# First feed-forward block of a decoder trunk: raw tokens enter, the RMS scale is applied behind the first products

## The chip, the cores and the metric

The kernel runs on one core of one Trainium2 chip. The metric is the device time of one execution in microseconds; the kernel before takes 1079.5 us (median of three runs, 1079.46 to 1080.34).

## The reference, cut to what matters

One layer of a hybrid decoder: feed-forward, token mixer, feed-forward, on 16 meta tokens and 512 real tokens of width 1024. The change is in the first feed-forward alone:

```python
def rms_norm(x, g):
    ms = jnp.mean(xf * xf, axis=-1, keepdims=True)
    return xf * lax.rsqrt(ms + EPS) * g

def swiglu(h, w_in, w_out):
    gate, up = jnp.split(h @ w_in, 2, axis=-1)
    return (jax.nn.silu(gate) * up) @ w_out

h = jnp.concatenate([pad, meta, x], axis=1)
h = h + 0.5 * swiglu(rms_norm(h, ffn1_norm), ffn1_w_in, ffn1_w_out)   # d_ff = 2816
```

Two things follow from these lines. The factor 1/rms belongs to a token, so it can be put on a token's column of the product `h @ w_in` as well as on the token itself. And the sum needs the raw `h` a second time, as the residual.

## The kernel before, in words

**Numbers and products.** Everything is float32. TensorE works on "fp32r" operands, so each matrix is split into a high part (a rounded copy, made by ScalarE in `hi`, L134/L135) and a low part (the remainder, made by VectorE in `lo`, L141/L143). One product is then three matmuls: high by high (L302), low by high (L303), high by low (L305), 128 x 128 weights against 264 columns of tokens. Weights are split in the same way as they come in (`raw` to `wh` and `wl`).

**Layout.** Activations stand turned, features on partitions and 528 tokens (16 + 512) along the row: `hT` is 128 x 8 x 528. The tokens come in five tiles `xt` (one of 16, four of 128 tokens), are turned by TensorE's transposes (L668) into PSUM tiles called `ps` and `pt`, and are copied out in two halves: the first 264 columns are "token 0", the last 264 "token 1"; features 0 to 511 and 512 to 1023 are the two feature halves. A11, A12, A21, A22 are the four blocks (token, feature).

**Units.** The first projection is done in 22 units of 128 gate columns and 128 up columns. Units 0 and 1 are "plain" (`Units.plain`, L482): 8 block products each, that is 96 matmuls a unit and 192 in the two. Units 2 to 21 use seven products in place of eight (`Units.seven`, L519, 84 matmuls); they need sums of the blocks, made by `Halves.sums` (L434): S3 = A11 - A21, S1 = A21 - A22, S2 = S1 - A11, S4 = A12 + S2, each a 128 x 1056 VectorE operation and then split in two parts of 128 x 1056. Their weights come as sums too, part of which the accumulating DMA of GpSimd's queue (L212) forms, and part VectorE (`tc`, L234 and L235).

**The entry before.** A token tile is squared and summed (L635, L636), 1/rms comes from a small VectorE operation (`entry_rms`, L650) and a power on GpSimd (L352), and the tile is scaled in place (`entry_scale`, L660) before it is turned. So `hT` holds normalised tokens (with the gain), and the raw tokens are loaded a second time while units 4 to 6 run (`fetch`, L795) and turned again to become the residual (`residual` and `turn`, L810 to L819: 40 transposes and 10 copies). TensorE runs 20 matmuls on an identity matrix first (L346) while the loads are under way.

**What sets the order.** A scheduler orders each engine's instructions when the program is built, from the order of the code and from the buffers; on the chip each engine takes its queue strictly in that order, and waits at an instruction whose operands or buffers aren't ready. `inline` (L619) ties entry operations of one engine to each other. PSUM has four `ps` and four `pt` tiles. The weight tiles `raw`, `wh` and `wl` have three buffers each, the tiles for added weights (`rawC`, `rawD`) two.

## Time and profile before

| what | value |
|---|---|
| median of three runs | 1079.5 us |
| the profiled execution's own time | 1080.09 us |
| its span, first to last instruction | 1078.3 us |
| mean granted TensorE clock | 1.000 |
| busy: TensorE, VectorE, ScalarE, GpSimd | 1069.0, 893.2, 656.6, 195.9 us |
| TensorE's share of the chain that ended last | 89% |

In the profile PE is TensorE's matmuls, PEld its weight loads, DVE VectorE, ACT ScalarE, POOL GpSimd, and SP the engine that issues most loads. A row of the timeline gives start, duration, engine, line, operation, tiles and count; a part in brackets is idle time before it and what ended it. Durations overlap by some hundredths of a microsecond on a busy engine, so the step from one start to the next is an instruction's cost there; for a matmul of 264 columns, whose row says 0.28 us, that step is about 0.122 us.

### The profile page before, as it was taken

Reading aid. Unit: us, or ns where it says so; the run is one execution under the profiler, and the core shown is the slowest. Engines: PE = TensorE matmul, PEld = TensorE weight load, DVE = VectorE, ACT = ScalarE, POOL = GpSimd, SP = SyncE. Lnnn points to the kernel's source line nnn. Section 1 sums busy time; section 2 is a strip of 40 time slices with the busy share of each in tenths; the row PEclk is TensorE's granted clock in tenths of the full one; section 3 lists DMA queues with packets and bytes.
Section 4 is the critical chain, followed back from the end, with each engine's and each line's share of the span. In section 5 each row is a group of like instructions: output and inputs, shape, how many; then the busy total and the mean of one; then the engine's idle time right before and its main releaser. Section 6 shows DMA issues by size and latency. Waiting matters only on the chain.

```text
span 1078.3 us, 22318 instructions
## 1 busy us (share of the span) xinstructions
PE 1069.0 (99%) x8579; PEld 1037.4 (96%) x8579; DVE 893.2 (83%) x1718; ACT 656.6 (61%) x1243; POOL 195.9 (18%) x233
## 2 busy tenths in 40 slices
PE   9999999999999999999999999999999999999998
PEld 8999999999999999999978799999999999999998
DVE  7988878888889677788897799788998788887895
ACT  7667456656666455556667866555666466645664
POOL 3011111121124430221200110001122211221120
PEclk9999999999999999999999999999999999999999
DMA  7787788688786423112211775467688777887763
GB/s 267 212 213 166 189 192 196 152 222 213 177 179 174 121 75 124 48 53 74 74 52 60 232 178 139 173 199 199 174 203 176 191 187 184 180 192 193 161 123 103
DMA packets 111723, 173.06 MB, mean 160 GB/s; under 512 B 10800, under 2 KB 58160, under 8 KB 111232
## 3 DMA queue, kind: packets, MB, share of 16 engines
q1 hardware_dynamic: 74032, 122.03, 35.9%
q0 software_dynamic: 28768, 37.83, 22.6%
q10 hardware_dynamic: 8816, 11.77, 3.3%
q8 instruction: 67, 1.10, 0.4%
q14 instruction: 40, 0.33, 0.1%
HBM read 167.37 MB, written 6.32 MB: 161 GB/s over the span
## 4 chain that ended last, share of the span: by engine, by line
PE 89%; DVE 6%; ACT 3%; issue 1%; DMA 1%; POOL 0%; ACTq 0%; SPq 0%; DVEq 0%; POOLq 0%
PE ps L302 15%; PE ps L305 15%; PE ps L303 15%; PE pt L302 12%; PE pt L303 12%; PE pt L305 12%; DVE wl L141 1%; ACT t L1189 1%; ACT wh L134 1%; DMA raw<-in_wg_dram 1%; PE ps L346 1%; DVE pL L141 1%; PE pt L1229 1%; PE pt L1274 1%; PE ps L1396 0%
## 5 line engine op out<-in xcount | busy, mean ns | idle before, releaser
L302 PE MATMUL ps<-x,wh 128*128 128x256 f32 (+2 forms) x768 | 219.7, 286 | 0.2
L303 PE MATMUL ps<-x,wh 128*128 128x256 f32 (+2 forms) x768 | 218.9, 285 | 0.5 <-DVE x L143 0.4
L305 PE MATMUL ps<-x,wl 128*128 128x256 f32 (+2 forms) x768 | 218.9, 285 | 0.0
L141 DVE TENSOR_TENSOR wl<-raw,wh 128x1024 fp32r<-128x1024 f32 (+3 forms) x125 | 150.1, 1202 | 44.5 <-ACT wh L134 43.2
L134 ACT CAST wh<-raw 128x1024 fp32r<-128x1024 f32 (+3 forms) x125 | 128.5, 1029 | 88.0 <-PE ps L303 57.4
L302 PEld LDWEIGHTS ps<-x,wh 128*128 128x128 f32 x768 | 144.8, 189 | 1.7 <-ACT hT L687 0.3
L303 PEld LDWEIGHTS ps<-x,wh 128*128 128x128 f32 x768 | 144.5, 188 | 1.4 <-DVE x L143 0.9
L305 PEld LDWEIGHTS ps<-x,wl 128*128 128x128 f32 x768 | 144.6, 188 | 0.9
L302 PE MATMUL pt<-x,wh 128*128 128x256 f32 (+2 forms) x424 | 125.3, 296 | 0.2 <-ACT wh L134 0.2
L305 PE MATMUL pt<-x,wl 128*128 128x256 f32 (+2 forms) x424 | 124.5, 294 | 0.0
L303 PE MATMUL pt<-x,wh 128*128 128x256 f32 (+2 forms) x392 | 112.5, 287 | 0.0
L134 ACT CAST wh<-tc 128x1024 fp32r<-128x1024 f32 (+1 forms) x70 | 71.8, 1026 | 64.5 <-DVE tc L235 57.1
L141 DVE TENSOR_TENSOR wl<-tc,wh 128x1024 fp32r<-128x1024 f32 (+1 forms) x70 | 83.5, 1193 | 32.4 <-ACT wh L134 32.1
L302 PE MATMUL ps<-acts,wh 128*128 128x264 f32 (+1 forms) x352 | 100.5, 285 | 0.1
L305 PE MATMUL ps<-acts,wl 128*128 128x264 f32 (+1 forms) x352 | 99.9, 284 | 0.0
L303 PE MATMUL ps<-acts,wh 128*128 128x264 f32 (+1 forms) x352 | 99.5, 283 | 0.0
L141 DVE TENSOR_TENSOR wl<-rawC,wh 128x1024 fp32r<-128x1024 f32 (+1 forms) x70 | 84.2, 1202 | 5.8 <-ACT wh L134 5.5
L134 ACT CAST wh<-rawC 128x1024 fp32r<-128x1024 f32 (+1 forms) x70 | 71.6, 1023 | 22.8 <-PE pt L303 17.8
L302 PEld LDWEIGHTS pt<-x,wh 128*128 128x128 f32 x424 | 79.9, 189 | 2.6 <-ACT wh L134 0.5
L305 PEld LDWEIGHTS pt<-x,wl 128*128 128x128 f32 x424 | 79.7, 188 | 2.1
L303 PEld LDWEIGHTS pt<-x,wh 128*128 128x128 f32 x392 | 73.8, 188 | 0.6
L302 PEld LDWEIGHTS ps<-acts,wh 128*128 128x128 f32 x352 | 66.5, 189 | 0.7 <-DVE h2T L919 0.3
(427 smaller groups left out, 3248.4 us busy)
## 6 DMA issues: line engine op xcount, KB each, us to landing
rawC<-in_w1i_dram SPq DMA_DIRECT2D x20, 512.0 KB, 4.7
raw<-in_w1i_dram SPq DMA_DIRECT2D x40, 256.0 KB, 4.7
raw<-in_w2i_dram SPq DMA_DIRECT2D x40, 256.0 KB, 3.4
rawC<-in_w2i_dram SPq DMA_DIRECT2D x20, 512.0 KB, 4.4
raw<-in_wm_dram SPq DMA_DIRECT2D x18, 512.0 KB, 4.5
raw<-in_wout_dram SPq DMA_DIRECT2D x16, 512.0 KB, 4.1
rawD<-in_w1i_dram SPq DMA_DIRECT2D x20, 256.0 KB, 4.7
raw<-in_w1i_dram POOLq DMA_DIRECT2D x20, 256.0 KB, 4.9
```

Of the source, the lines that this page charges most:

```text
L134: return A.copy(o, i)
L141: return V.tensor_tensor(out=o, in0=i, in1=h, op=ALU.subtract)
L302: PE.matmul(ps, sH, mH, start=first, stop=False, **more)
L303: PE.matmul(ps, sH, mL, start=False, stop=False, **more)
L305: shared["mm"] = PE.matmul(ps, sL, mH, start=False, stop=last, **more)
L346: PE.matmul(idle[:, :P], ident, ident, start=True, stop=True)
L1189: shared["exp"] = A.activation(t, t, AF.Exp, bias=nmx, scale=-1.0, accum_out=l[:, j : j + 1])
L1229: PE.matmul(ps[:, :w], q[qx][hb, hp, P * i : P * i + P], k[kx][hb, hp, c0 : c0 + w], start=qx + kx == 0, stop=qx == 1 and not last,)
L1274: PE.transpose(ps[:, c : c + P], ts_[hh][(c // P) % 2][:, c0 : c0 + P], ident)
```

## The change

Tokens are turned raw. The copies of the turned tokens (`hT`) carry no gain and no scale, so `hT` is the residual from the start, and `fetch`, `residual`, `turn` and their 40 transposes and second loads are gone. The blocks A11 to A22 that the two plain units use are split from raw tokens times gain. The factor 1/rms is spread over partitions into a new tile `rb0` (128 x 528) by a product with the identity (`spread_r`, with `spread` of L361: 5 matmuls, 2 copies). A plain unit's gate goes out of PSUM through a VectorE multiplication with `rb0`, then Silu, then a GpSimd multiplication with `rb0` (which stands for the up side's factor), and then as before. For the units of seven products the normalised tokens are made in a new tile `xn`, feature by feature (`normal`: ScalarE with the gain, GpSimd with `rb0`), and A11, A22 and A12 are split again from it (`again`); the sums follow from `xn`.

```diff
 def plain(...):
+                    s = box[t] = self.new("s", 3)
+                    z = ps[:, :th]
+                    if by is not None:
+                        V.tensor_tensor(out=s, in0=z, in1=by[:, c], op=ALU.mult)
+                        z = s
+                    A.activation(s, z, AF.Silu)
+                    if by is not None:
+                        G.tensor_tensor(out=s, in0=s, in1=by[:, c], op=ALU.mult)
...
 def keep(k, eng):
-            inline(("A", lambda: A.activation(o, src, AF.Identity, scale=g)))
+            inline(("A", lambda: A.copy(o, src)))
...
 def enter_first():
-        inline(("A", lambda: entry_square(0, "A")), ("V", lambda: entry_square(1, "V")), ("V", lambda: entry_rms(0, 2)))
-        inline(("V", lambda: entry_scale(1, "V")))
...
+        inline(("A", lambda: entry_square(1, "A")), ("V", lambda: entry_square(2, "V")), ("A", lambda: entry_square(0, "A")))
+        G.tensor_copy(wh[:, half[1]], raw[:, half[1]])
         pss1.update(zip(range(7), to_features(0, range(7))))
         features(0)
+        inline(("A", lambda: hi(wh[:, half[0]], raw[:, half[0]])), rest[0])
         features(1)
...
 def enter_rest():
+        inline(("V", lambda: entry_rms(0, 3)))
+        spread_r((0, 1, 2))
...
         inline(("A", lambda: entry_square(3, "A")), ("A", lambda: entry_square(4, "A")))
+        inline(("V", lambda: entry_rms(3, 5)))
+        spread_r((3, 4))
...
+    def normal(k):
+        x_ = shared["xn"][:, k]
+        A.activation(x_, hT[:, k], AF.Identity, scale=gT[:, 0, k : k + 1])
+        G.tensor_tensor(out=x_, in0=x_, in1=rb0, op=ALU.mult)
...
+    u0, u1 = (ff1.plain(act1(u), False, rb0) for u in range(2))
+    run(u0[:1] + [enter_rest] + u0[1:4] + [lambda: enter_second(range(4))] + u1[:1])
+    run([lambda: enter_second(range(4, KD))] + u1[1:2] + [loaded])
+    fresh = [lambda k=k: normal(k) for k in range(KD)]
+    s3, s1, s2, s4 = X.sums()
+    run(weave(u0[4:6] + u1[2:4], fresh))
+    again = lambda n, t, f: lambda: X.again(n, X.of(t, f))
+    run(u0[6:8] + [again("A11", 0, 0), s3] + u1[4:5] + [s1] + u1[5:6] + [s2] + u1[6:8])
+    run([again("A22", 1, 1), again("A12", 0, 1), s4])
```

The order that the scheduler makes of it differs at three places. Rows are line, operation, output and input tiles, size and count.

The first place is the entry, where tiles 3 and 4 (`xt_80` and `xt_81`) are turned. On TensorE's queue before, the 60th of the plain units' matmuls (the fourth row) stands ahead of them:

```order
L305 MATMUL ps_313<-x_190,wl_238 128x264
L302 MATMUL ps_313<-x_190,wh_237 128x264
L303 MATMUL ps_313<-x_191,wh_237 128x264
L305 MATMUL ps_313<-x_190,wl_238 128x264
L668 MATMUL pt_326<-ident,xt_80 128x128
L668 MATMUL ps_327<-ident,xt_80 128x128
L668 MATMUL pt_328<-ident,xt_80 128x128
L668 MATMUL ps_329<-ident,xt_80 128x128
L668 MATMUL pt_326<-ident,xt_81 128x128
L668 MATMUL ps_327<-ident,xt_81 128x128
L668 MATMUL pt_328<-ident,xt_81 128x128
L668 MATMUL ps_329<-ident,xt_81 128x128
```

Now only the 24 matmuls of unit 0's gate on token 0 (two block products) and three transposes stand between the first tiles' transposes and this piece, and in it are the products that spread 1/rms (`rin`) over the partitions, L369; the last of them, for tiles 3 and 4, stands ahead of unit 0's up side (`ps_286`):

```order
L749 MATMUL pt_312<-ident,xt_80 128x128
L749 MATMUL pt_312<-ident,xt_81 128x128
L369 MATMUL ps_233<-ident,rin 128x16
L369 MATMUL ps_233<-ident,rin 128x128 x2
L749 MATMUL pt_312<-ident,xt_80 128x128
L749 MATMUL pt_312<-ident,xt_81 128x128
L749 MATMUL pt_351<-ident,xt_80 128x128
L749 MATMUL pt_351<-ident,xt_81 128x128
L749 MATMUL pt_351<-ident,xt_80 128x128
L749 MATMUL pt_351<-ident,xt_81 128x128
L369 MATMUL ps_253<-ident,rin 128x128 x2
L302 MATMUL ps_286<-x_181,wh_221 128x264
```

So 36 matmuls that stood ahead of the second half's transposes stand behind them, and behind the second spreading product.

On ScalarE's queue at the same place, from the first big weight cast to the squares of tiles 3 and 4 (`sq`), before:

```order
L134 CAST wh_228<-raw_93 128x1024
L135 ACTIVATE x_222<-pt_167,gT 128x264
L135 ACTIVATE x_222<-pt_218,gT 128x264
L687 ACTIVATE hT<-ps_162,gT 128x272
L134 CAST wh_237<-raw_97 128x1024
L687 ACTIVATE hT<-ps_164,gT 128x272
L635 ACTIVATE sq_29_245,rin<-xt_80 128x1024
L635 ACTIVATE sq_30_247,rin<-xt_81 128x1024
L687 ACTIVATE hT<-ps_166,gT 128x272
L687 ACTIVATE hT<-pt_218,gT 128x272
L501 ACTIVATE s_267<-ps_205 128x264
```

and now:

```order
L134 CAST wh_221<-raw_93 128x1024
L135 ACTIVATE x_215<-pt_159,gT 128x264
L694 COPY hT<-ps_154 128x272
L135 ACTIVATE x_215<-pt_211,gT 128x264
L134 CAST wh_238<-raw_97 128x1024
L694 COPY hT<-ps_156 128x272
L694 COPY hT<-ps_158 128x272
L134 CAST wD_651<-rawD_282 128x512
L694 COPY hT<-pt_211 128x272
L647 ACTIVATE sq_30_247,rin<-xt_80 128x1024
L647 ACTIVATE sq_31_249,rin<-xt_81 128x1024
L511 ACTIVATE s_269<-s_269 128x264
```

Two more copies of `hT` and the cast of `wD` have come ahead of the two squares. Further up, the cast of half of the first weight (`wh_144`) has moved from ahead of the first `x` part to behind it; GpSimd casts the other half now.

The second place is GpSimd's queue and ScalarE's behind the plain units. GpSimd's queue now, where before only the power (L352) and accumulating loads (L212) stood:

```order
L352 TENSOR_TENSOR rin<-rin,nhalf 128x2
L212 DMA raw_277<-in_w1i_dram 128x512
L513 TENSOR_TENSOR s_269<-s_269,rb_139 128x264
L212 DMA rawC_281<-in_w1i_dram 128x512
L212 DMA raw_632<-in_w1i_dram 128x512
L212 DMA rawC_654<-in_w1i_dram 128x512
L763 TENSOR_TENSOR xn<-xn,rb_139 128x528
L513 TENSOR_TENSOR s_385<-s_385,rb_139 128x264
L763 TENSOR_TENSOR xn<-xn,rb_139 128x528 x2
L513 TENSOR_TENSOR s_433<-s_433,rb_139 128x264
L763 TENSOR_TENSOR xn<-xn,rb_139 128x528 x5
L212 DMA raw_750<-in_w1i_dram 128x512
```

ScalarE's queue now, where `x_181` is A11's high part, `x_215` A12's, `x_357` A22's, `x_519` S3's, and `wh_444` the second weight of unit 2:

```order
L134 CAST wh_333<-raw_277 128x1024
L134 CAST x_215<-xn 128x1056
L134 CAST wh_444<-tc_441 128x1024
L134 CAST acts_399<-sums_509 128x264
L134 CAST x_519<-sum_517 128x1056
L134 CAST x_357<-xn 128x1056
L542 COPY pt_614<-ps_613 128x264
L134 CAST wh_628<-rawC_281 128x1024
L134 CAST x_538<-sum_536 128x1056
L511 ACTIVATE s_554<-s_554 128x264
```

The eight multiplications of `xn` and the four of `s` (three of them are in these rows) are new on GpSimd, and on ScalarE the splits of S3 and A22 stand behind the high part of A12, which reads the last four features of `xn`.

The third place is VectorE's queue from the low part of unit 2's second weight (before `wl_477`, now `wl_445`) to that of its third (`wl_594`, now `wl_629`). Before:

```order
L141 TENSOR_TENSOR wl_477<-tc_473,wh_476 128x1024
L431 TENSOR_TENSOR acts_428<-hT,acts_428 128x1056
L504 TENSOR_TENSOR u_312<-pt_543,s_536 128x264
L141 TENSOR_TENSOR x_508<-acts_428,x_507 128x1056
L141 TENSOR_TENSOR x_540<-acts_428,x_539 128x1056
L832 TENSOR_TENSOR sums_461<-u_204,u_312 128x264
L141 TENSOR_TENSOR acts_460<-u_312,acts_460 128x528
L832 TENSOR_TENSOR sums_461<-sums_461,u_204 128x264
L141 TENSOR_TENSOR wl_594<-rawC_277,wh_593 128x1024
```

Now, in two pieces, in which `x_520`, `x_539`, `x_561` are the low parts of S3, S1 and S2, and `x_358` and `x_216` those of A22 and A12:

```order
L141 TENSOR_TENSOR wl_445<-tc_441,wh_444 128x1024
L141 TENSOR_TENSOR acts_399<-sums_509,acts_399 128x264
L141 TENSOR_TENSOR x_520<-sum_517,x_519 128x1056
L436 TENSOR_TENSOR sum_536<-xn 128x1056
L509 TENSOR_TENSOR s_554<-pt_523,rb_139 128x264
L436 TENSOR_TENSOR sum_558<-sum_536,xn 128x1056
L141 TENSOR_TENSOR x_539<-sum_536,x_538 128x1056
L516 TENSOR_TENSOR u_337<-pt_564,s_554 128x264
L141 TENSOR_TENSOR x_358<-xn,x_357 128x1056
L141 TENSOR_TENSOR x_561<-sum_558,x_560 128x1056
```

```order
L830 TENSOR_TENSOR sums_508<-u_197,u_337 128x264
L141 TENSOR_TENSOR acts_399<-u_337,acts_399 128x528
L830 TENSOR_TENSOR sums_508<-sums_508,u_197 128x264
L141 TENSOR_TENSOR x_216<-xn,x_215 128x1056
L141 TENSOR_TENSOR acts_399<-sums_508,acts_399 128x528
L830 TENSOR_TENSOR sums_509<-u_337,sums_508 128x264
L436 TENSOR_TENSOR sum_603<-xn,sum_558 128x1056
L141 TENSOR_TENSOR acts_399<-sums_509,acts_399 128x264
L141 TENSOR_TENSOR wl_629<-rawC_281,wh_628 128x1024
```

Nine rows have become nineteen: the splits of A22 and A12 are new, and S3, two sums and S1 have come in between.

More of the change, by code (lines that the diff above doesn't have):

```diff
@@ L810, in residual @@
-    def residual(i):
-        c, n = ttile[i]
-        for hf in range(2):
-            turn(again[i][hf], c, n, hf, psum())
-    def turn(xr, c, n, hf, ps):
-        for k in range(4):
-            PE.transpose(ps[:, k * n : k * n + n], xr[:n, k * P : k * P + P], ident[:n, :n])
-        A.copy(hT[:, 4 * hf : 4 * hf + 4, c : c + n], ps[:, : 4 * n].rearrange("p (k c) -> p k c", c=n))
     got = {}
@@ L925 @@
         for u in range(max(2 * j0, NC[0]), 2 * (j0 + n)):
[L926 to L934 removed]
+            ff1.unit(act1(u), u == 2 * (j0 + n) - 1)
             if u >= 8 and u < 16:
```

142 lines of the change are left out of this document (61 added, 81 removed).

## The prediction

> **What bounds the kernel now.** I read the page first, then the stretches of the first 50 us, then TensorE's timeline there. The page's row of busy times:
>
> ```profile
> PE 1069.0 (99%) x8579; PEld 1037.4 (96%) x8579; DVE 893.2 (83%) x1718; ACT 656.6 (61%) x1243; POOL 195.9 (18%) x233
> ```
>
> TensorE bounds the whole: it is busy for 99% of the span. A microsecond of its work that goes is gained, and a microsecond in which it waits is lost, wherever it lies. So the question is what the change takes from TensorE, and whether the stage it rebuilds still feeds TensorE. That stage, by stretches (window, then PE, PEld, DVE, ACT and POOL busy, clock, DMA):
>
> ```profile
> 10.00:20.00 10.00, 9.40 (x72) 8.40 (x72) 7.95 (x17) 9.26 (x21) 1.73 (x4) 1.00 0.97 363
> 20.00:30.00 10.00, 9.98 (x80) 9.19 (x79) 9.99 (x20) 7.08 (x18) 3.74 (x4) 1.00 0.60 109
> 30.00:40.00 10.00, 10.00 (x84) 10.00 (x84) 10.00 (x14) 5.22 (x7) 1.71 (x2) 1.00 0.74 205
> 40.00:50.00 10.00, 9.94 (x82) 9.73 (x81) 10.00 (x16) 6.24 (x12) 0.00 (x0) 1.00 0.77 215
> ```
>
> VectorE is as full as TensorE from 20 to 50 us. TensorE hardly waits, but VectorE has nothing to spare: what is added to its queue, or holds it up, in these 30 us comes out at TensorE. TensorE's timeline, with the warming matmuls, the first transpose, the 60th of the 264-column matmuls, the first behind the second half's transposes, the bias table's pair up to the next product, the 144th, the 192nd (as many as the plain units have) and the 289th (unit 2's first on `wD`):
>
> ```profile
> 1.47 7.68 PE L346 MATMUL ps<-ident 128*128 128x128 f32 x40 [1.47 <-POOL ident masks.py:199]
> 8.99 0.27 PE L668 MATMUL pt<-ident,xt 128*128 128x128 f32 x1
> 20.57 0.28 PE L305 MATMUL ps<-x,wl 128*128 128x264 f32 x1
> 22.97 0.37 PE L302 MATMUL ps<-x,wh 128*128 128x264 f32 x1
> 24.52 0.39 PE L752 MATMUL ps<-ohr,tbH 128*32 128x512 f32 x1
> 24.97 0.28 PE L302 MATMUL pt<-acts,wh 128*128 128x264 f32 x1
> 33.62 0.29 PE L305 MATMUL ps<-x,wl 128*128 128x264 f32 x1
> 39.49 0.28 PE L305 MATMUL pt<-x,wl 128*128 128x264 f32 x1
> 51.62 0.28 PE L302 MATMUL pt<-x,wD 128*128 128x264 f32 x1
> ```
>
> From the 144th to the 192nd are 48 steps in 5.87 us: 0.122 us for a matmul, the price I use throughout.
>
> **Gain: the residual's transposes.** The 40 transposes leave TensorE, these 36 and four more of a meta tile:
>
> ```profile
> L818 PE MATMUL ps<-ident,acts x36: 208/272/273, 69.1 to 86.5; 128*128 128x128 f32 x32, 16*128 16x16 f32 x4
> 9.10 0.27 PE L668 MATMUL ps<-ident,xt 128*128 128x128 f32 x1
> 9.21 0.27 PE L668 MATMUL pt<-ident,xt 128*128 128x128 f32 x1
> 10.05 0.21 PE L668 MATMUL ps<-ident,xt 16*128 16x16 f32 x1
> 10.12 0.21 PE L668 MATMUL pt<-ident,xt 16*128 16x16 f32 x1
> ```
>
> The durations overlap; the steps are 0.11 us for a full tile and 0.06 us for a meta tile: 32 x 0.11 + 8 x 0.06 = 4.0 us, all on the path. Ten copies on ScalarE and the second loads go too; no wait of TensorE is put down to them, so I count nothing.
>
> **No gain at the front.** The first tiles aren't scaled any more. But the warming matmuls hold TensorE to 9.15 us (1.47 + 7.68), and before, the first transpose followed them at once: scaling was hidden behind them. It starts at 9.0 again.
>
> **Loss at the entry.** Unit 0's up side now stands behind the products that spread 1/rms of tiles 3 and 4, and so behind their squares:
>
> ```profile
> 17.79 1.07 ACT L635 ACTIVATE sq<-xt 128x1024 f32<-128x1024 f32 x1
> 18.74 0.21 ACT L635 ACTIVATION_READ_ACCUMULATOR sq<-xt 128x1 f32 x1
> 18.83 0.49 ACT L687 ACTIVATE hT<-ps,gT 128x272 f32<-128x272 f32 x1
> 19.20 0.50 ACT L687 ACTIVATE hT<-pt,gT 128x272 f32<-128x272 f32 x1
> 18.98 0.17 DVE L650 TENSOR_SCALAR rin<-rin 128x2 f32<-128x2 f32 x1
> 19.23 0.71 POOL L352 TENSOR_TENSOR rin<-rin,nhalf 128x2 f32<-128x2 f32 x1 [4.93 <-DVE rin L650]
> 7.83 1.14 ACT L134 CAST wh<-raw 128x512 fp32r<-128x512 f32 x2 [0.27 <-DMA raw<-in_w1i_dram]
> ```
>
> The squares end at 18.95. ScalarE works without a gap from the first `x` part at 10.74 on (9.26 us busy in the stretch from 10 to 20), and now has ahead of that point one half cast (1.14 / 2 = 0.57), the cast of `wD` of the same size (0.57) and two more copies (2 x 0.37, the step from 18.83 to 19.20): 1.9 us more, so 20.8. From the squares' end to the power's end it was 19.94 - 18.95 = 1.0 us, so 21.8; two spreading products of two passes each (the 20 warming matmuls show as 40; 0.11 a pass, as a transpose's) and hand-overs of 0.2: the up side starts at 22.4. At 22.97 before, 60 matmuls and all 16 transposes were behind TensorE; now 24 matmuls and 8 transposes are, with 168 and 8 ahead, and the pair on the bias table (L752, 24.52 to 24.97, 0.45): 22.4 + 20.5 + 0.9 + 0.45 = 44.2 us for the plain units' end, against 39.6. **Loss so far 4.6 us.** Spreading itself is in it.
>
> **Loss at the sums.** `xn` needs GpSimd, which worked on tiles of 128 x 528 in one group of rows before (shown with its dearest and its cheapest, and with the landing time of the accumulating loads in its queue):
>
> ```profile
> L897 POOL TENSOR_TENSOR sqacc<-sqacc,u 128x528 f32<-128x528 f32 x5 | 8.3, 1659 | 0.8 <-ACT u L896 0.8
> 351.95 1.89 POOL L897 TENSOR_TENSOR sqacc<-sqacc,u 128x528 f32<-128x528 f32 x1 [0.26 <-ACT u L896]
> 358.58 1.33 POOL L897 TENSOR_TENSOR sqacc<-sqacc,u 128x528 f32<-128x528 f32 x1
> raw<-in_w1i_dram POOLq DMA_DIRECT2D x20, 256.0 KB, 4.9
> ```
>
> That is the form and size of the eight `xn` multiplications: 1.66 us in the mean, 1.33 at least, 1.89 at most. The four of half the size aren't in the trace; I take half the mean, 0.83, between the halves of the ends, 0.67 and 0.95. GpSimd starts when ScalarE has the first `xn`, which stands in its queue behind the last copy of the second half. The transposes for that stand behind 36 matmuls: 22.4 + 4.4 + 0.9 = 27.7. The copy takes 0.6 (half of a 1024-column cast, and a little), two parts 0.7 (two of the steps of 0.37 each), the first `xn` 0.6 and hand-overs the rest: 29.6. Eight full and two half multiplications end at 29.6 + 13.3 + 1.7 = 44.6. Only then can ScalarE cast A12's high part, and behind it in its queue stands the second weight's of like size:
>
> ```profile
> 29.30 2.05 ACT L134 CAST x<-acts 128x1056 fp32r<-128x1056 f32 x2
> ```
>
> Two such casts take 2.05, less the tenth by which they overlap the next: 46.5. (Behind `xn` stand accumulating loads of units 4 and on in GpSimd's queue; unit 4 begins with the 361st matmul, at 75 us by what follows, and a load lands in 4.9, so they have 20 us to spare. SP's loads wait for buffers that VectorE frees, and move with it.) Then VectorE's nineteen rows of the third place:
>
> ```profile
> 31.16 1.24 DVE L141 TENSOR_TENSOR x<-acts,x 128x1056 fp32r<-128x1056 f32 x1
> 32.32 0.41 DVE L504 TENSOR_TENSOR u<-pt,s 128x264 f32<-128x264 f32 x1
> 32.67 1.20 DVE L141 TENSOR_TENSOR wl<-raw,wh 128x1024 fp32r<-128x1024 f32 x1
> 33.80 0.42 DVE L832 TENSOR_TENSOR sums<-u 128x264 f32<-128x264 f32 x1
> ...
> 43.72 0.70 DVE L141 TENSOR_TENSOR acts<-u,acts 128x528 fp32r<-128x528 f32 x1
> 44.34 0.43 DVE L832 TENSOR_TENSOR sums<-sums,u 128x264 f32<-128x264 f32 x1
> ```
>
> By steps from start to start, 1.16 for 1056 columns, 1.13 for 1024, 0.35 for 264, 0.62 for 528: 8 x 1.16 + 2 x 1.13 + 7 x 0.35 + 2 x 0.62 = 15.2 us, so 61.7. The last of them is the low part of unit 2's third weight, and TensorE's next product needs it: by its queue the 249th matmul. Without a wait TensorE would be there at 44.2 + 57 x 0.122 = 51.1. So it stands still for some 10.6 us between 45.6 and 61.7. Forty matmuls on, the 289th starts at 61.7 + 4.9 = 66.6, and 0.2 later for the weight that VectorE splits next; before it was at 51.62. **Loss in all 15.2 us**, the entry's 4.6 in it. VectorE's own bill is smaller (three added low parts, 3.5 us, four multiplications and two copies, 2.2 at the price of 264 columns, against five scalings that go); what costs is that the sums wait for GpSimd, and VectorE's work bunches behind them.
>
> **GpSimd against VectorE.** Rows in which the two overlap:
>
> ```profile
> 337.74 2.26 DVE L143 SCALAR_TENSOR_TENSOR x<-hT,gT,x 128x528 fp32r<-128x528 f32 x1
> 342.98 1.85 POOL L897 TENSOR_TENSOR sqacc<-sqacc,u 128x528 f32<-128x528 f32 x1
> 344.08 1.82 DVE L141 TENSOR_TENSOR wl<-raw,wh 128x1024 fp32r<-128x1024 f32 x1
> ```
>
> A VectorE split of 1.2 us took 1.82 in one place, and one of 528 columns, 0.70 by the rows above, took 2.26 in another, so a GpSimd multiplication costs VectorE 0.6 to 1.6 us; what it costs GpSimd is in the mean of 1.66. I take 0.6, from the row that is nearest in kind. Four `xn` meet VectorE while it has work (39 to 44.6 us): 2.4 us, of which 2.0 lie in VectorE's wait for the cast at 46.5 (its rows end near 44.5 otherwise). I add 0.4, or 4 x 1.6 - 2.0 = 4.4 by the other row. The Trainium skill ("SBUF — State Buffer", on who interferes with whom) says why: a VectorE instruction with two SBUF inputs and a GpSimd instruction that reads SBUF exclude each other for the whole instruction. By that rule four multiplications and VectorE's rows of that time alternate without any overlap, and I would add some 1.8, an estimate from its text; the rows above agree that one of the two waits.
>
> **The sum:** 15.2 + 0.4 - 4.0 = +11.6 us. The profiled execution's own 1080.09 us becomes 1091.7, the median's 1079.5 becomes **1091.1 us**. Bounds: with GpSimd at 1.33 the sums' chain starts 2.0 us earlier, where VectorE's queue before it ends, giving +9.6; with 1.89 and the dearer row, 1.9 and 4.0 us more, +17.5.
>
> **Rivals.**
> (1) *Covered at the sums.* If the chain from GpSimd to the 249th matmul came in time, the entry's 4.6 and the gain of 4.0 would be left: 1080.1 us. It would take 10 us less in a chain of which VectorE's 15.2 us are the most; VectorE's full stretches speak against it.
> (2) *Faster.* The entry's wait is where the sign is decided: were ScalarE's squares of tiles 3 and 4 done before TensorE has ended the 24 matmuls and three transposes (about 17.5 us), nothing would stand at L369, and with a covered chain the change would be 1079.5 - 4.0 + 1.0 (spreading: eight passes of 0.11, two of 0.06) = 1076.5 us. For it speaks that ScalarE is busy only 61%; against it, its queue at the entry, which has no gap. It decides as soon as both places together lose less than 3.0 us besides the spreading.
> (3) *A slower TensorE behind the wait.* The 40 warming passes step by 7.68 / 40 = 0.19 us, a transpose's pass by 0.11: TensorE is slow at first. If standing still brings that back, a stretch as long as that first one loses up to 7.68 x (1 - 0.11 / 0.19) = 3.3 us: 1094.4 us. For it speaks that the wait at the sums, 10 us in two or three pieces, is of the length of the start; against it, that no later row shows such a thing. The Trainium skill ("TensorE: Matmul & The Clock Gate", Part 1) has such a gate: half the rate after an idle window of about 3.4 us, the full rate after as long a busy one. By it the loss would be about 1.7 us a time, an estimate from that page; no row of the profile before shows an idle stretch of that length behind the start.
>
> **How the numbers follow.** The chain as summed: 0.74 (1089.1 to 1097.0). Rival 3: 0.13. Rival 1: 0.06. Rival 2: 0.07. Slower by over 0.2% (2.2 us, about what a measurement here can tell from no change): 0.87; within: 0.06; faster: 0.07. The range leaves out rivals 1 and 2 and a little of the dear end, where every overlap would have to cost what the dearest row shows: it goes to 1096.5; at the cheap end it goes 2.6 us below the bound, to 1086.5, since the steps of half-size operations and hand-overs are estimates.
>
> **What would show it.** Right: TensorE's first transpose at 9.0; a wait of 4 to 5 us ahead of L302 on `ps`, from about 17.5 to 22.4, with GpSimd's power as its releaser; the plain units' end at 44; 1.3 to 1.9 us for L763; in the stretch from 45 to 62 TensorE busy for about 6 us, waits on VectorE's low parts; `wD`'s first product at 66 to 69; no L818, and from 70 us on the same steps as before. Wrong: a `wD` product before 58, or a TensorE without waits between 45 and 62.

## The result, and the profile after

The changed kernel takes **1098.42 us** (median of 6 runs, 1097.02 to 1098.77) against 1079.70 us before (6 runs beside it, 1079.46 to 1080.54): a ratio of 1.0169, 95% interval 1.0156 to 1.0182, or 18.7 us more. The forecast had the sign and the place, but 11.6 us as the size, and a range that ends at 1096.5.

The profiled execution took 1097.02 us, span 1095.2 us, against a span of 1078.3 us before: 16.9 us more. It is the fastest of the six, so the two traces account for 16.9 of the 18.7 us.

The stretches of the changed kernel (window, then PE, PEld, DVE, ACT and POOL busy, granted clock, DMA share, GB/s):

```profile
10.00:20.00 10.00, 7.16 (x39) 5.89 (x40) 7.62 (x16) 8.90 (x20) 3.42 (x4) 0.91 1.02 405
20.00:30.00 10.00, 8.86 (x60) 8.46 (x59) 6.17 (x15) 4.31 (x10) 5.15 (x6) 0.75 0.67 106
30.00:40.00 10.00, 10.00 (x81) 9.68 (x80) 4.74 (x8) 8.32 (x15) 7.90 (x7) 1.00 0.30 90
40.00:50.00 10.00, 7.54 (x63) 7.33 (x61) 9.46 (x10) 4.24 (x6) 8.35 (x5) 1.00 0.32 93
50.00:60.00 10.00, 6.52 (x28) 5.39 (x29) 9.37 (x12) 7.31 (x10) 2.57 (x2) 0.79 0.24 40
60.00:70.00 10.00, 7.85 (x40) 7.43 (x39) 8.32 (x12) 3.50 (x7) 0.00 (x0) 0.70 0.21 66
```

Two things are new. VectorE, full from 20 us on before, is half idle from 20 to 40 us and full only then. And the granted clock is 0.75 from 20 to 30 us and 0.79 and 0.70 from 50 to 70 us, in stretches that hold a wait of TensorE and the work behind it; before, it was 1.00 in all of these stretches. TensorE's "busy" of 6.5 us from 50 to 60 us holds only 28 matmuls, over half of them at half the rate (0.22 us from start to start in place of 0.12).

TensorE's timeline, with the warming matmuls, the first transpose, both waits at L369, the first up matmul and a later one, the two first of S3 in unit 2, the 249th product with one behind it, and the first on `wD`:

```profile
1.47 6.21 PE L346 MATMUL ps<-ident 128*128 128x128 f32 x40 [1.47 <-POOL ident masks.py:199]
7.52 0.27 PE L672 MATMUL pt<-ident,xt 128*128 128x128 f32 x1
...
17.89 1.53 PE L369 MATMUL ps<-ident,rin 16*128 16x16 f32 x6 [1.50 <-POOL rin L352]
...
21.84 1.23 PE L369 MATMUL ps<-ident,rin 128*128 128x128 f32 x4 [1.14 <-POOL rin L352]
22.71 0.57 PE L302 MATMUL ps<-x,wh 128*128 128x264 f32 x1
...
24.62 0.42 PE L305 MATMUL ps<-x,wl 128*128 128x264 f32 x1
...
50.91 0.39 PE L302 MATMUL ps<-x,wh 128*128 128x264 f32 x1 [3.36 <-ACT x L134]
52.40 0.59 PE L303 MATMUL ps<-x,wh 128*128 128x264 f32 x1 [1.10 <-DVE x L141]
...
65.72 0.39 PE L305 MATMUL pt<-x,wl 128*128 128x264 f32 x1 [1.81 <-DVE wl L141]
...
66.31 0.42 PE L305 MATMUL pt<-x,wl 128*128 128x264 f32 x1
...
72.25 0.28 PE L302 MATMUL pt<-x,wD 128*128 128x264 f32 x1
```

The first product on `wD` was at 51.62 us and is at 72.25, 20.6 us later. Take off the residual's transposes, which are gone behind it (3.9 us, measured below), and 16.7 remain: the whole difference of the spans lies ahead of this product.

The engines that TensorE waits for, in the order of time. The first four rows are the end of ScalarE's squares and what VectorE does ahead of the second L662, the row that GpSimd's second power waits for:

```profile
18.93 0.19 ACT L647 ACTIVATION_READ_ACCUMULATOR sq<-xt 128x1 f32 x1
19.45 0.44 DVE L371 COPY rb<-ps 128x272 f32<-128x272 f32 x1 [2.37 <-PE ps L369]
19.81 0.78 DVE L696 COPY hT<-pt 128x272 f32<-128x272 f32 x2
20.51 0.42 DVE L509 TENSOR_TENSOR s<-ps,rb 128x264 f32<-128x264 f32 x1
20.84 0.16 DVE L662 TENSOR_SCALAR rin<-rin 128x2 f32<-128x2 f32 x1
21.08 0.70 POOL L352 TENSOR_TENSOR rin<-rin,nhalf 128x2 f32<-128x2 f32 x1 [3.25 <-DVE rin L662]
...
32.10 1.32 POOL L763 TENSOR_TENSOR xn<-xn,rb 128x528 f32<-128x528 f32 x1 [5.87 <-ACT xn L762]
...
38.38 9.14 POOL L763 TENSOR_TENSOR xn<-xn,rb 128x528 f32<-128x528 f32 x5
...
40.87 1.46 DVE L141 TENSOR_TENSOR x<-xn,x 128x1056 fp32r<-128x1056 f32 x1 [0.51 <-ACT x L134]
42.25 2.35 DVE L141 TENSOR_TENSOR wl<-raw,wh 128x1024 fp32r<-128x1024 f32 x1
44.52 1.81 DVE L234 TENSOR_TENSOR tc<-rawC,rawD 128x512 f32<-128x512 f32 x1
46.26 0.42 DVE L516 TENSOR_TENSOR u<-pt,s 128x264 f32<-128x264 f32 x1
46.60 1.47 DVE L235 TENSOR_TENSOR tc<-tc,rawC 128x512 f32<-128x512 f32 x1
...
47.55 1.07 ACT L134 CAST x<-xn 128x1056 fp32r<-128x1056 f32 x1 [5.76 <-POOL xn L763]
...
49.60 1.23 DVE L141 TENSOR_TENSOR wl<-tc,wh 128x1024 fp32r<-128x1024 f32 x1
...
64.45 1.22 DVE L141 TENSOR_TENSOR wl<-rawC,wh 128x1024 fp32r<-128x1024 f32 x1
```

The last row is the split that the 249th product waits for. In the kernel before, VectorE's first sum and the same split stood here:

```profile
27.34 1.24 DVE L431 TENSOR_TENSOR acts<-hT 128x1056 f32<-128x1056 f32 x1
...
44.68 1.22 DVE L141 TENSOR_TENSOR wl<-rawC,wh 128x1024 fp32r<-128x1024 f32 x1
```

This gives a ledger. From the first row that reads a whole block of normalised tokens (128 x 1056) to the end of that split VectorE took 45.90 - 27.34 = 18.6 us before, and 65.67 - 40.87 = 24.8 us after. So the block begins 13.5 us later and is 6.2 us longer: 19.8 us. From its end to the `wD` product it was 5.7 us, and is 6.6: 0.9 more. The experiments test the parts of these numbers.

### The profile page after: what moved, and what is told of

It reads as the page before. It is cut to its first block, busy times and chain, and to the rows that moved or that the text cites. A ratio compares the mean times of both kernels' runs of the same rounds, so it can differ in the third digit from the quotient of the medians.

```text
span 1095.2 us, 22270 instructions
## 1 busy us (share of the span) xinstructions
PE 1074.7 (98%) x8549; PEld 1040.9 (95%) x8549; DVE 900.1 (82%) x1719; ACT 659.7 (60%) x1240; POOL 215.7 (20%) x245
## 4 chain that ended last, share of the span: by engine, by line
PE 87%; DVE 6%; ACT 3%; issue 1%; POOL 1%; DMA 1%; ACTq 0%; DVEq 0%; POOLq 0%
PE ps L302 15%; PE ps L305 15%; PE ps L303 15%; PE pt L302 12%; PE pt L303 12%; PE pt L305 12%; DVE wl L141 1%; ACT t L1183 1%; ACT wh L134 1%; DMA xg<-h1d 1%; PE ps L346 1%; POOL xn L763 1%; PE pt L1223 1%; PE pt L1268 1%; DVE pL L141 0%
## 5 line engine op out<-in xcount | busy, mean ns | idle before, releaser
L302 PE MATMUL ps<-x,wh 128*128 128x256 f32 (+2 forms) x768 | 222.3, 290 | 4.7 <-ACT x L134 3.6
L303 PE MATMUL ps<-x,wh 128*128 128x256 f32 (+2 forms) x768 | 221.0, 288 | 2.4 <-DVE x L141 1.6
L141 DVE TENSOR_TENSOR wl<-raw,wh 128x1024 fp32r<-128x1024 f32 (+3 forms) x125 | 151.4, 1212 | 44.6 <-ACT wh L134 43.3
L302 PEld LDWEIGHTS ps<-x,wh 128*128 128x128 f32 x768 | 146.6, 191 | 6.9 <-ACT x L134 4.0
L303 PEld LDWEIGHTS ps<-x,wh 128*128 128x128 f32 x768 | 146.4, 191 | 3.9 <-DVE x L141 2.0
L302 PEld LDWEIGHTS ps<-acts,wh 128*128 128x128 f32 x352 | 66.5, 189 | 0.6 <-DVE h2T L921 0.3
```

The lines of the kernel that those rows point to most:

```text
L141: return V.tensor_tensor(out=o, in0=i, in1=h, op=ALU.subtract)
L302: PE.matmul(ps, sH, mH, start=first, stop=False, **more)
L303: PE.matmul(ps, sH, mL, start=False, stop=False, **more)
```

## The experiments

The theory: TensorE loses at two places, at the entry behind the spreading of 1/rms, and at the sums behind a chain that goes from GpSimd's `xn` through ScalarE's casts to VectorE's rows; a slow clock behind the waits adds to it. The rivals: VectorE is full, whoever makes `xn`; GpSimd costs by making VectorE's rows longer, not by being waited for; the clock alone; and a gain that is smaller than thought. Each kernel has its own median of before beside it; the difference to that is what is compared.

| kernel | median us | before us | difference | ratio (95%) |
|---|---|---|---|---|
| changed kernel | 1098.42 | 1079.70 | +18.7 | 1.0169 (1.0156 to 1.0182) |
| e1 no residual | 1076.03 | 1079.89 | -3.9 | 0.9965 (0.9952 to 0.9977) |
| e2 xn on VectorE | 1094.16 | 1079.89 | +14.3 | 1.0133 (1.0118 to 1.0148) |
| e3 xn unscaled | 1094.06 | 1079.89 | +14.2 | 1.0131 (1.0116 to 1.0146) |
| e4 late spread | 1095.20 | 1079.89 | +15.3 | 1.0141 (1.0126 to 1.0156) |
| e5 late, VectorE | 1093.07 | 1080.35 | +12.7 | 1.0114 (1.0100 to 1.0128) |
| e6 VectorE, once | 1091.37 | 1080.35 | +11.0 | 1.0104 (1.0091 to 1.0118) |
| e7 stirred | 1098.60 | 1080.35 | +18.3 | 1.0167 (1.0153 to 1.0181) |
| e8 rescaled | 1076.84 | 1080.35 | -3.5 | 0.9966 (0.9953 to 0.9978) |
| e9 idle GpSimd | 1101.43 | 1080.03 | +21.4 | 1.0201 (1.0187 to 1.0215) |
| e10 stirred last | 1096.55 | 1080.03 | +16.5 | 1.0152 (1.0139 to 1.0166) |
| e11 raw sums | 1090.96 | 1080.03 | +10.9 | 1.0099 (1.0084 to 1.0115) |
| e12 late, VectorE, once | 1088.31 | 1080.03 | +8.3 | 1.0078 (1.0066 to 1.0091) |

The intervals reach 1.3 to 1.7 us to either side, so two rows that differ by less than some 2 us are told apart by their traces, if at all.

One thing runs through the traces with the new entry. From the end of the last split to the `wD` product they show 5.2 to 5.3 us in e3, e4, e9, e10 and e11, and 6.5 to 7.8 in the changed kernel, e2, e5, e6, e7 and e12, where matmuls behind the wait step by 0.22 us; only in e10 was the full clock intended. So 1.3 us or more of a difference between two rows can be the clock behind the last wait. How it falls from one execution of a kernel to the next was not measured.

**e1, the gain alone.** The kernel before without its residual:

```
-            between = {4: {"P7": does(fetch, 1, 2, 0, 3)}, ...}
-            ff1.unit(act1(u), u == 2 * (j0 + n) - 1, between)
-            for f in {4: [does(residual, 1), does(fetch, 4)], ...
+            ff1.unit(act1(u), u == 2 * (j0 + n) - 1)
```

> This is the kernel before without its 40 residual transposes, their copies and the second fetch of the tokens (the residual then stays the normalised tokens, so part of the output is left out). It measures the gain term alone. By the forecast's sum: 4.0 us less than the kernel before, 1075.7 us. If the transposes lay in TensorE's idle time anyway (the change saves nothing, and all the loss is smaller than it looks): 1079.7 us.

Measured 3.9 us less. The gain is real and of the size that the steps of 0.11 and 0.06 us gave (4.0). So the new entry costs 18.7 + 3.9 = 22.6 us, not 15.6.

**e2, xn on VectorE.**

```
-        A.activation(x_, hT[:, k], AF.Identity, scale=gT[:, 0, k : k + 1])
-        G.tensor_tensor(out=x_, in0=x_, in1=rb0, op=ALU.mult)
+        V.scalar_tensor_tensor(out=x_, in0=hT[:, k], scalar=gT[:, 0, k : k + 1], in1=rb0,
+                               op0=ALU.mult, op1=ALU.mult)
```

> The changed kernel with each of the eight parts of xn made by one VectorE instruction in place of one on ScalarE and one on GpSimd. Theory (the chain GpSimd, ScalarE, VectorE behind xn sets when the 249th matmul can go): ScalarE's cast of the second half no longer waits 5.8 us for GpSimd, VectorE pays about 8 x 0.7 us in 30 to 45 us where it is idle about half the time, so 3 to 5 us come back: 1093.5 to 1095.5 us. Rival (VectorE is simply too full in 40 to 66 us; whoever multiplies does not matter): VectorE gets 5.6 us more, no gain or a loss of up to 5.6: 1098.4 to 1104 us.

Measured +14.3, or 4.4 less than the changed kernel, in the theory's range, although VectorE got eight rows more. Its timeline:

```profile
36.74 3.30 DVE L762 SCALAR_TENSOR_TENSOR xn<-hT,gT,rb 128x528 f32<-128x528 f32 x4
...
40.65 1.24 DVE L141 TENSOR_TENSOR x<-xn,x 128x1056 fp32r<-128x1056 f32 x1
...
42.19 1.23 DVE L141 TENSOR_TENSOR wl<-raw,wh 128x1024 fp32r<-128x1024 f32 x1
...
60.89 1.22 DVE L141 TENSOR_TENSOR wl<-rawC,wh 128x1024 fp32r<-128x1024 f32 x1
```

Each `xn` costs 0.7 to 0.8 us, in a time in which VectorE had been half idle. The splits that took 1.46 and 2.35 us beside GpSimd take 1.24 and 1.23. The block begins hardly earlier (40.65 us in place of 40.87) and is 3.3 us shorter, and nearly all of that is the four rows of two SBUF inputs that stood beside GpSimd (7.1 us there, 3.9 here). So this run takes away the wait for GpSimd and the stretching together, and cannot tell the one from the other. From `x<-xn` to the end of the last split it is still 21.5 us of rows with one pause of 0.6: taking GpSimd out does not free VectorE.

**e3, GpSimd's multiplications left out.** The second of the two lines above that e2 removes goes, and nothing takes its place.

> The changed kernel without GpSimd's eight multiplications of xn by 1/rms (xn then lacks that factor in units 2 to 21). Theory (chain behind xn): ScalarE's cast is free 5.8 us earlier and VectorE's rows are no longer stretched by GpSimd (some 3 us), together 6 to 9 us: 1089.5 to 1092.5 us. Rival (VectorE too full, GpSimd hidden): 1096 to 1098.4 us, only the stretch of VectorE's rows at most coming back.

Measured +14.2: 4.5 us less, where the theory had 6 to 9 and the rival 0 to 2.4. Both miss. That the work on `xn` costs nothing here (e3) or eight VectorE rows (e2) makes no difference that the runs can tell, though 1.3 us of e3's gain can be the clock behind the last wait; what ends last behind it is the same in both:

```profile
41.50 1.26 DVE L141 TENSOR_TENSOR x<-xn,x 128x1056 fp32r<-128x1056 f32 x1
...
62.20 1.22 DVE L141 TENSOR_TENSOR wl<-rawC,wh 128x1024 fp32r<-128x1024 f32 x1
```

Again 21.9 us of rows, with pauses of 1.0 us in all, from 41.5 us on. So GpSimd's share is 4.4 us, and behind it VectorE stands as the bound: the last split ends at 62.1 us in e2 and at 63.4 in e3, 16.2 and 17.5 us later than before (45.90).

**e4, the second spreading late.**

```
         inline(("V", lambda: entry_rms(3, 5)))
-        spread_r((3, 4))
...
-    run(u0[:1] + [enter_rest] + u0[1:4] + [lambda: enter_second(range(4))] + u1[:1])
+    run(u0[:1] + [enter_rest] + u0[1:4] + [lambda: enter_second(range(4)), lambda: spread_r((3, 4))] + u1[:1])
```

> The changed kernel with the spreading of 1/rms of the last two token tiles put behind 24 matmuls of the up side, on TensorE, in place of ahead of them. Theory (the wait at the entry is on the path, and everything behind it moves with it): the wait of 2.6 us and the slow clock behind it (1.3 us) go, and the start of xn moves with them: 1094.5 to 1095.5 us. Rival (what TensorE loses at the entry it would only wait for at the sums instead, since the sums wait for GpSimd and VectorE): 1097.5 to 1098.4 us.

Measured +15.3: 3.4 us less, in the theory's range. In its profiled execution the up side starts at 19.78 us in place of 22.71, but GpSimd's first `xn` only 0.35 us earlier (31.75) and the end of the last split 0.3 (65.40), behind a first transpose that was 1.1 us later; the stretch behind the split is 1.3 us shorter, at the full clock. So the entry's second wait is on the path, and `xn` moves with it by less than the wait; how much of the 3.4 us is the wait's own stays open.

**e5, both together.**

> The changed kernel with both earlier edits together: the spreading of the last two tiles' 1/rms behind 24 up matmuls, and xn on VectorE. If the entry's wait and GpSimd's chain are two separate losses that lie one behind the other: 1098.4 - 3.2 - 4.3, about 1091 us (1090.3 to 1091.8). Rival (with xn on VectorE its rows run from 32 to 66 us almost without a pause, so an earlier entry only makes TensorE wait longer for them): 1093 to 1094.2 us.

Measured +12.7: 6.0 us less than the changed kernel, where the sum of the two is 7.8. By the median it is the edge of the rival's range, by the difference to before it lies between the two. The losses lie one behind the other for the most part; with the intervals as they are, that a part of the second is hidden by the first is neither shown nor excluded.

**e6, no second split.** Over e2:

```
-    run(u0[6:8] + [again("A11", 0, 0), s3] + u1[4:5] + [s1] + u1[5:6] + [s2] + u1[6:8])
-    run([again("A22", 1, 1), again("A12", 0, 1), s4])
+    run(u0[6:8] + [s3] + u1[4:5] + [s1] + u1[5:6] + [s2] + u1[6:8])
+    run([s4])
```

> The changed kernel with xn on VectorE and without the second split of A11, A12 and A22 (three casts of 1.07 us on ScalarE, three residues of 1.25 us on VectorE left out; the products then take halves without 1/rms, so the output differs). Theory (behind GpSimd stands VectorE: 19 rows of 15 us end last, three of them these): 3.75 us less than with xn on VectorE alone (1094.2): 1090 to 1091 us. Rival (behind GpSimd it is TensorE's own rows at the slow clock, or the split of the weights): 1093.5 to 1094.5 us.

Measured +11.0, 3.3 us less than e2 for three rows of 1.25 us (3.5 by their steps); three casts on ScalarE go with them. Rows taken out of VectorE's block come out at the end almost one for one, and nothing else steps in: VectorE's queue sets the time here.

**e7, idle matmuls in unit 2.**

```
             c = psum()
+            stir(c, 14)
             product(c, "S3", w, 1)
...
             d = psum(True)
+            stir(d, 10)
             A.activation(d[:, :th], b[:, :th], AF.Identity, scale=-1.0)
```

The ten write into the tile that later products add to, so what is summed there changes, not what is issued.

> The changed kernel with 24 idle matmuls of the identity in unit 2: 14 ahead of S3 (in the wait of 3.5 us) and 10 in the wait ahead of the 249th product. Theory (the granted clock is low behind these waits and the matmuls after 65.7 us go at 0.22 us instead of 0.12 for some 3.7 us): TensorE comes out of the wait at the full clock, 0.7 to 1.7 us less, 1096.7 to 1097.7 us. Rival (the clock is no loss of its own; what waits is VectorE's rows): 1098.2 to 1099.2 us.

Measured +18.3: no difference. The trace shows why, and that this run was no test of the clock behind the last wait: the clock was full from 47 to 63 us and bought nothing, since TensorE only waited longer (2.3 us instead of 1.8) for the same split; and then, with no idle matmul left for the last pause (the ten had run from 53.9 to 60.6 us), it fell all the same:

```profile
65.83 0.39 PE L305 MATMUL pt<-x,wl 128*128 128x264 f32 x1 [2.26 <-DVE wl L141]
...
66.68 0.42 PE L303 MATMUL pt<-x,wh 128*128 128x264 f32 x1
```

**e8, the gain without the new entry.** The kernel before, with the residual computed in place:

```
+    def unscale():
+        again["place"] = t = last_acts().rearrange("p a b c -> p (a b c)").bitcast(F32)
+        again["rms"], inv = t[:, :T], t[:, T : T + NB + 1]
+        again["ig"] = t[:, T + 8 : T + 8 + KD]
+        V.reciprocal(inv, rin)
+        V.reciprocal(again["ig"], gT[:, 0])
+        spread(inv, [(i,) + ttile[i] for i in range(NB + 1)], again["rms"])
+
+    def residual(k):
+        V.scalar_tensor_tensor(out=hT[:, k], in0=hT[:, k], scalar=again["ig"][:, k : k + 1],
+                               in1=again["rms"], op0=ALU.mult, op1=ALU.mult)
```

> The kernel before with its normalised entry, but with the residual won back in place in units 5 and 6, by eight VectorE instructions (normalised token times rms over gain; it needs gains that are not zero) in place of the second fetch, the 40 transposes and the ten copies. If the change's gain can be had without its entry: 3.9 us less for the transposes, 1 us more for five matmuls that spread the rms: 1076.5 to 1077.5 us. Rival (the eight instructions, two at a time, hold up VectorE's pieces of units 5 and 6 and TensorE waits): 1078.5 to 1081 us.

Measured 3.5 us less than before, ratio 0.9966 (0.9953 to 0.9978): faster than both kernels. The eight calls stand two at a time in units 5 and 6, in place of the second fetch, the transposes and the copies. They are 6.0 us of VectorE, none of which comes out at the end, since the gain is that of e1 within the intervals:

```profile
L804 DVE SCALAR_TENSOR_TENSOR hT<-hT,acts 128x528 f32<-128x528 f32 x8 | 6.0, 758 | 0.0
```

It holds only for gains that are not zero.

**e9, GpSimd works for nobody.** e2, in which GpSimd does its eight multiplications all the same:

```
+        G.tensor_tensor(out=shared["dm"], in0=x_, in1=rb0, op=ALU.mult)
```

> The kernel with xn on VectorE (1094.2 us measured), in which GpSimd does eight multiplications of the same form all the same, into a tile that nobody reads. Nobody waits for GpSimd's result here; what is left of its cost is only that it makes VectorE's rows longer. If the stretched rows are what GpSimd's part cost (three rows of 0.7 to 1.2 us took 1.5 to 2.4 us beside it in the changed kernel, some 3 to 4 us together, and VectorE has no pause there): 1096.5 to 1098.5 us. Rival (ScalarE's wait of 5.8 us for GpSimd's last part was the cost): 1094 to 1095 us.

Measured +21.4: 7.1 us more than e2, and more than the changed kernel itself. Nobody waits for these multiplications, and VectorE has no pause from 32 to 61 us, so the whole price is that the two engines hold each other up:

```profile
36.13 2.35 DVE L141 TENSOR_TENSOR wl<-raw,wh 128x1024 fp32r<-128x1024 f32 x1
38.40 6.52 DVE L764 SCALAR_TENSOR_TENSOR xn<-hT,gT,rb 128x528 f32<-128x528 f32 x4
...
42.56 9.58 POOL L765 TENSOR_TENSOR sum<-xn,rb 128x528 f32<-128x528 f32 x5
...
48.65 0.42 DVE L516 TENSOR_TENSOR u<-pt,s 128x264 f32<-128x264 f32 x1
```

Four `xn` take 6.52 us in place of 3.30, a split 2.35 in place of 1.21; GpSimd takes 1.92 us for a multiplication that took 1.32 alone. The row with one input in PSUM (L516) takes 0.42 us beside GpSimd as without it. The Trainium skill ("SBUF — State Buffer", on who interferes with whom) says that a VectorE instruction with two SBUF inputs and a GpSimd instruction that reads SBUF exclude each other, and that a VectorE instruction with at most one SBUF input, outside the two-port modes, does not contend. The trace agrees on which rows are held up. It does not show a full exclusion: VectorE's `xn` came every 1.61 us and GpSimd's multiplications every 1.9, alone they take 0.81 and 1.30, and 0.81 / 1.61 + 1.30 / 1.9 is 1.2, more than one. What the wait for GpSimd costs without the stretching was not run.

**e10, idle matmuls in the last wait.** Nine of them, on TensorE's queue directly ahead of the 249th product:

```
+        if state.get("stir") is not None:
+            b = state.pop("stir")
+            with tc.issue_after(getattr(mm, "ins", mm)):
+                for _ in range(9):
+                    mm = PE.matmul(b[:, :P], ident, ident, start=True, stop=True)
```

> The changed kernel with nine idle matmuls put directly ahead of the 249th product on TensorE's queue, so that they run in its last wait. If the slow clock behind that wait is a loss of its own (some 14 matmuls at 0.22 in place of 0.12 us): 1.2 to 1.5 us less than the changed kernel, about 1097 us, and steps of 0.12 us behind the wait in the trace. If the clock's price there is made up later: 1098.4 us.

Measured +16.5, 2.2 us less; by the intervals hardly more than nothing, so the steps carry it:

```profile
64.88 2.17 PE L309 MATMUL ps<-ident 128*128 128x128 f32 x18
66.80 0.37 PE L313 MATMUL pt<-x,wl 128*128 128x264 f32 x1
67.01 0.28 PE L302 MATMUL pt<-x,wh 128*128 128x264 f32 x1
...
71.80 0.29 PE L302 MATMUL pt<-x,wD 128*128 128x264 f32 x1
```

From the 249th product to the `wD` product it takes 71.80 - 66.80 = 5.0 us, against 72.25 - 65.72 = 6.5 in the changed kernel. The clock behind the last wait is worth 1.5 us, less the 0.2 by which the idle matmuls held that product back behind its split (66.56 to 66.80). Behind the earlier waits of unit 2 it bought no earlier split (e7), since TensorE only reached the next wait sooner; behind the last one stands work that is ready.

**e11, sums from the raw tokens.** Over e4:

```
     def normal(k):
-        ...
+        pass
...
-        X.xn = shared["xn"] = ep.tile([P, KD, T], F32, name="xn")
+        X.xn = hT
```

> The changed kernel with the late spreading, and with the sums and second splits taken from the raw tokens: xn isn't made at all (units 2 to 21 then lack gain and 1/rms). Theory (VectorE's rows of the sums start some 9 us late because xn is, and then stand end to end; xn itself is 5.7 us of VectorE or a GpSimd chain): against the kernel with the late spreading and xn on VectorE (1093.1) 4 to 5.5 us less, 1087.5 to 1089 us. Rival (what the plain units' own pieces wait for holds VectorE at 39 to 41 us whoever makes xn): 1091.5 to 1093 us.

Measured +10.9, 1.8 us less than e5. The theory (4 to 5.5) fails; the 1091.0 us lie between the two ranges, 0.5 below the rival's. By the traces the last split ends 1.3 us earlier than in e5, and the stretch behind it, at the full clock here, is 1.3 us shorter. With `xn` free, VectorE's block still begins only at 38 us, behind a pause of 2.7:

```profile
36.92 1.08 ACT L134 CAST x<-hT 128x1056 fp32r<-128x1056 f32 x1 [2.52 <-PE ps L305]
38.03 1.26 DVE L141 TENSOR_TENSOR x<-hT,x 128x1056 fp32r<-128x1056 f32 x1 [2.69 <-ACT x L134]
...
39.55 0.42 DVE L516 TENSOR_TENSOR u<-pt,s 128x264 f32<-128x264 f32 x1
39.89 1.25 DVE L436 TENSOR_TENSOR sum<-hT 128x1056 f32<-128x1056 f32 x1
...
58.99 1.22 DVE L141 TENSOR_TENSOR wl<-rawC,wh 128x1024 fp32r<-128x1024 f32 x1
```

VectorE waits for ScalarE's cast of A11, and that cast for TensorE: `again` writes the second split of A11 into the tiles that the plain units' products still read. In e2 and e5 the same cast waits 2.8 us for the same products. `sums` orders the first sum behind this split, so it begins at 39.9 us, where before the first one began at 27.34. It is their place behind the plain units, not only the making of `xn`, that starts the sums late. Tiles of its own for the second split, which would take this tie away, were not tried.

**e12, all three.** e5 without the second splits.

> The changed kernel with the late spreading, xn on VectorE and no second split of A11, A12 and A22 (those products then lack 1/rms). If the three losses add, as rows in one queue do: 1093.1 less 3.0, 1089.5 to 1090.7 us. If without the second splits another wait stands there (the weights' split, or TensorE itself): 1091.5 to 1093 us.

Measured +8.3, 4.4 us less than e5, more than either expectation had (the rows' own price is 3.5). VectorE's block:

```profile
31.34 1.43 DVE L761 SCALAR_TENSOR_TENSOR xn<-hT,gT,rb 128x528 f32<-128x528 f32 x2
...
56.87 1.22 DVE L141 TENSOR_TENSOR wl<-rawC,wh 128x1024 fp32r<-128x1024 f32 x1
```

From 31.34 to 58.09 it takes 26.8 us against 18.6 before (5.4 of them are the eight `xn`), and starts 4.0 us later: 12.2 us at its end. The `wD` product comes at 65.84 in this execution, 14.2 us later than before; the other 2.0 are the stretch behind the 249th product, at the slow clock until 64.2 us. Less the gain of 3.9 that makes 10.3, and this execution's span is 9.7 us longer than before's (1088.0 against 1078.3); the median of the five is 1.4 us better than that. None of the repairs comes near the kernel before.

## Why the prediction had the sign and not the size

**The bound and the gain: right.** What TensorE lost ahead of the `wD` product came out at the end (16.7 of the 16.9 us between the spans), and the transposes were worth 3.9 us (forecast 4.0).

**No gain at the front: wrong for this execution, and of no use.** The forecast held the first transpose at 9.0 us, behind 7.68 us of warming. The warming took 6.21 us in the profiled execution, and the first transpose ran at 7.52. The 40 passes are the same in every kernel here, and their row took 6.21 to 7.68 us; so this is the execution's, not the change's. The lead was lost again at L369.

**Loss at the entry: the start right by luck, on the wrong engine.** The up side began at 22.71 us (forecast 22.4), by e4 up to 3.4 us of it on the path. But the squares, by which the forecast reckoned (20.8), had ended at 19.12, 2.0 us before GpSimd's power began; 1.5 us of that is the earlier first transpose. What the power waited for was VectorE's L662, at 20.84, and that stood in VectorE's queue behind the copies and the first multiplication that need the *first* spreading. Two spreadings in one queue, the second behind the first's consumers: the forecast followed ScalarE's queue and not VectorE's. The lead at the front and this wait, neither of which it had, cancelled. The plain units then ended at 45.9 us, not at 44.2.

**Loss at the sums: here the prediction failed, in the cause and in three terms.** The cause: it held VectorE's own bill to be the smaller part, and said that "what costs is that the sums wait for GpSimd". With GpSimd out of the way 4.4 of the 22.6 us come back (e2, e3), and the last split still ends 16 us later than before. What the runs showed in its place is VectorE's own queue: its rows begin late whoever makes `xn`, behind the plain units' products (e11), stand end to end from there, and rows taken out of it come out at the end almost one for one (e6). The terms: on the way from 29.6 to 61.7 us the forecast lost 4.0, since the split ended at 65.67.

- *xn starts at 32.1, not 29.6: 2.5 of the 4.0 us.* Behind the entry's wait the up matmuls went at 0.22 us (the row at 24.62 and those before it) until 25 us, 1.0 us lost; 0.3 comes from the up side's start, and 0.9 from ScalarE behind the last transposes: two parts took 0.92 in place of 0.7, an `xn` 0.74 in place of 0.6, and 0.4 ahead of it the trace does not explain. Another 0.3 stays open.
- *GpSimd's price, 0.4 us by the forecast.* GpSimd itself took 1.83 us for each of the last five, against 1.66, and ended at 47.5 (forecast 44.6): its eight full and two half multiplications took 0.4 us more than forecast, the rest is the later start. On VectorE the four rows of two SBUF inputs from 40.87 to 46.60 took 7.1 us, where the same four take 3.9 in e2. The forecast let 2.0 of its 2.4 us vanish in VectorE's wait for a cast at 46.5; there was no such wait, VectorE and the cast reached that point within 0.1 us of each other, both 3 us late. So here neither the stretched rows nor the late cast alone held up what follows. A multiplication cost VectorE 0.9 us (3.2 us over the 3.6 multiplications of that time; 7.1 us of time for eight in e9), between the forecast's 0.6 and its dearer 1.6.
- *VectorE's nineteen rows,* 15.2 us by the forecast, took 16.1 (49.60 to 65.67): 0.6 of it is a pause for GpSimd's half-size multiplication. That is 0.9 more; the last 0.2 lie at the casts.

**Rival 3 came true beside the forecast.** It was set against the forecast as a case of its own, with a chance of 0.13, though nothing in it excluded the chain. It was an addition: the clock fell behind the entry's wait (1.0 us by the steps) and behind the last one (1.3 to 1.5 us, e10). The forecast's sum has nothing for it. It belonged there, or at least in the range's dear end, which was cut at 1096.5 where the forecast's own bound stood at 1097.0.

**Rivals 1 and 2: wrong.** Nothing was covered at the sums. Even with the entry's second wait, GpSimd's chain and the second splits all taken away (e12) the change loses 8.3 us: VectorE's block still starts 4.0 us later than before and holds the eight `xn` and the plain units' added rows.

Together: 4.0 us at the split and 1.5 behind it make the `wD` product 5.5 us later than the forecast's 66.8, or 5.1 with the 0.4 that it added for GpSimd; the traces' difference is 16.9 instead of 11.6. The last 1.8 us, between the two profiled executions and the medians, no trace shows. The profiled executions of e3 and e6, which have the same entry, began their transposes 1.3 and 0.9 us later than the changed kernel's did, and 0.8 and 0.4 of that were left at the up side; this could be a part of it, but it was not measured on the changed kernel.

## What to carry to other kernels

Normalising can be put off behind a product only for those who use that product. Here half of the consumers, the sums and the second splits, needed the normalised tokens themselves, and got them later, over a broadcast and three engines, in the one stage where VectorE was full. A second split that is written into tiles still being read can begin no earlier than their last reader ends (e11). Before work is moved, write down the start and the length of the block on the fullest engine; both changes add up, and here, with what follows the block, they gave the difference of the spans to within a microsecond. To save a recomputation that is off the critical engine's way, undo the cheap step in place (e8) rather than reorder the entry.

## What the runs showed of the hardware

- GpSimd beside VectorE can cost far more than its own waits: eight multiplications of 128 x 528 for nobody cost 7.1 us (e9), nearly a microsecond each. The rows held up were those whose two inputs both lie in SBUF; a row with one input in PSUM took 0.42 us beside GpSimd as without it.
- The clock can fall after short pauses. In e7 TensorE had worked at the full clock for 5 us, paused for some 2.3, and went at 0.22 us from 66.5 to 69.6; a pause of 1.95 us ahead of 56.27 in the same run brought no slow steps. The Trainium skill ("TensorE: Matmul & The Clock Gate", Part 1) puts the idle window at about 3.4 us, free-running; the pause here was shorter, so a window that is idle only in part must be enough for it, or the window is shorter. The full clock came back 3.8 us after the work resumed in e7, and 6.1 us after in e12.
- A slow clock between two waits for another engine cost nothing that the run could tell (e7); behind the last wait it cost 1.3 to 1.5 us (e10).
